# Hybrid decoder layer on one core: the dilated q, k loads on ScalarE's queue, one group's weights loaded a stage earlier, other places for tiles

## Chip, core and metric

One core of a Trainium2 chip runs the whole program. The metric is device microseconds per execution. Engines: TensorE (PE, matmuls; PEld its weight loads), VectorE (DVE), ScalarE (ACT), GpSimd (POOL) and SyncE (SP, which only issues DMAs here). ScalarE and GpSimd also issue DMAs, each in its own instruction order.

## The reference

A decoder layer on x (1 x 1024 x 1024, float32):

```
h     = rms_norm(x, norm_mix_g);  proj = h @ w_in          # 1024 x 5896
dil   = proj[..., :2304]  as (q, k, v) x 3 groups x 4 heads x 64
fox   = proj[..., 2304:3840] as (q, k, v) x 8 heads x 64;  f_logit = next 8 columns + b_fgt
gates = sigmoid(the last 2048 columns + b_gate)
o_a   = three dilated causal window attentions (window, dilation) = (128,1), (512,4), (2048,16),
        with ALiBi bias, merged by a softmax over their log denominators
o_b   = causal attention with logits q.k/8 + c_t - c_s,  c = cumsum(log_sigmoid(f_logit))
x     = x + (g_a * (o_a @ w_dil_out) + g_b * (o_b @ w_fox_out)) @ w_out
gu    = rms_norm(x, norm_ffn_g) @ w_ffn_in                  # 2 x 2816 columns
x     = x + (silu(gu[..., :2816]) * gu[..., 2816:]) @ w_ffn_down
out   = rms_norm(x, norm_final_g)
```

## The kernel before

Every large matmul is done as three: operands are split into a high and a low part (`split`, L94: a copy on ScalarE, L95, and a subtraction on VectorE, L96), and `mm3` (L98) adds hi x hi, hi x lo and lo x hi in PSUM. A weight thus goes through a DMA into a raw tile (two buffers, tag "wr"), then ScalarE, then VectorE, then TensorE.

The stages, in order of time in the profile:

- 0 to 67 us, "foxv" (L349): x is loaded in 8 tiles of 128 rows, normalized (`norm_transpose`), transposed on TensorE and split into hT; `values` (L370) computes the fox values of one tile behind.
- 67 to 140, "dilv" (L424): weights w0 (dilated values of group 0 and the 8 forget columns, 264 columns) and w12 (groups 1 and 2, 512 columns) are loaded, split, and multiplied with the 8 row tiles, group 0 first; the staging tile `st` is stored to DRAM from ScalarE. Beside it, VectorE forms sums of quarters of hT (`form`, behind the last split of w12).
- 140 to 267, "proj" (L490): six calls of `projections`, each two columns blocks by a 2 x 2 block product with seven `prod` of 12 matmuls (L268) instead of eight. `left_side` (L254) makes its left operands: A1 and A22 are splits of raw weights; S12 and S34 are splits of sums that GpSimd forms in the tile `s`. `decay` (L452) turns the forget columns into the cumulated log gates.
- to about 511, "fox" (L535): fox attention, four head pairs. q and k lie in `ql`, `qx`, `kx` (two tiles of 4 KB each, one buffer).
- to 656, "dila" (L777): dilated attention in four units (head pair u, half b). `dil_qk` (L660) loads q, k of three groups, six tiles of 4 KB with one buffer each, from DRAM; `dil_scores` computes scores (L338, by `turns`) and VectorE adds the bias (L689 to L709); `dil_values` does exponentials (L739 to L745), values (L769) and denominators (L772), one unit behind.
- Filler: `ahead` (L214), 24 projections of 48 matmuls into two PSUM banks of their own, evacuated by ScalarE (L224); 8 for dilated q, k (L645), 16 for the gates (L793). They have no tie to the attention and are put wherever TensorE is free. The last one is tied behind the last dilated value matmul.
- then the merge (L802), w_out, the second norm, the first FFN product ("first", 2 plain column blocks, and from 881 "up", L954, 20 block products by `left_side`, `prod`), and the down projection.

The order on each engine is fixed before the run: the library's planner simulates the program with its own cost estimates and emits each engine's instructions in the order in which they became ready there, earlier program text first. At run time every engine works strictly in that order; an instruction that waits for a semaphore holds all behind it, DMA issues too. Memory is a stack of pools: a pool opened later takes the bytes of a closed one, tiles in the order of their first use, and a tile waits only for the users of earlier tiles on its own bytes. So in "proj" the tile `s` came to lie on w12, and in "dila" the six q, k tiles on ql, qx and kx.

Of the kernel before, what the change touches and what calls it, by code (L numbers as in the profile page):

```python
# [8 lines left out]
F32 = mybir.dt.float32  # L9
# [6 lines left out]
P = 128  # L16
# [31 lines left out]
def layer_kernel(  # L48
# [194 lines left out]
        nc.sync.dma_start(out=t[:], in_=src.rearrange("(k p) c -> p k c", p=P))  # L243
        return t

    def pair_of(raw, k=KT, pool=None, tag="w", bufs=2):

        pool = pool or wpool
        w = Pair(pool.tile([P, k, P], F32R, tag=tag + "h", name=nm("wh"), bufs=bufs),
                 pool.tile([P, k, P], F32R, tag=tag + "l", name=nm("wl"), bufs=bufs))  # L250
        split(w.hi[:], w.lo[:], raw)
        return w

    def left_side(pool, rg, ru, bufs):  # L254

        g1, g2, u1, u2 = rg[:, :4], rg[:, 4:], ru[:, :4], ru[:, 4:]
        A1 = pair_of(rg[:])
        s12 = pool.tile([P, KT, P], F32, tag="s", name=nm("s12"), bufs=2)
        nc.gpsimd.tensor_tensor(out=s12[:, :4], in0=u1, in1=u2, op=ALU.add)  # L259
        nc.gpsimd.tensor_tensor(out=s12[:, 4:], in0=s12[:, :4], in1=g1, op=ALU.subtract)  # L260
        S12 = pair_of(s12[:], KT, pool, "s12", bufs)
        s34 = pool.tile([P, KT, P], F32, tag="s", name=nm("s34"), bufs=2)
        nc.gpsimd.tensor_tensor(out=s34[:, :4], in0=g1, in1=u1, op=ALU.subtract)
        nc.gpsimd.tensor_tensor(out=s34[:, 4:], in0=g2, in1=s12[:, 4:], op=ALU.subtract)
        S34 = pair_of(s34[:], KT, pool, "s34", 1)
        return A1, S12, S34, pair_of(u2, 4, pool, "a22", 2)

    def prod(bank, a, b, first=False):  # L268
        for k in range(4):
# [5 lines left out]
    def projections(pool, T, c, dst, dls, sc):  # L275

        T1, T2, T3, T4 = T
        A1, S12, S34, A22 = left_side(pool, *[raw_w(w_in[:, c0:c0 + P]) for c0 in c], 1)
        b1, b2, b3 = pd(), pd(), pd()
        o1, o2 = [pool.tile([P, dl, S // dl], F32, tag="qo", name=nm("qo"), bufs=3) for dl in dls]  # L280
        n1, n2 = [HALF // dl for dl in dls]
        cc, v2, v3 = [pool.tile([P, HALF], F32, tag=n, name=nm(n), bufs=1) for n in ("cc", "v2", "v3")]

        def copy(out, bank, r=1):
            nc.scalar.activation(out=out, in_=view(bank[:], r), func=AF.Copy, scale=sc)

        def join(out, bank, other, r=1):
            p, q = view(bank[:], r), view(other[:], r)
            if sc == 1.0:
                nc.vector.tensor_tensor(out=out, in0=p, in1=q, op=ALU.add)  # L290
            else:
                nc.vector.scalar_tensor_tensor(out=out, in0=p, scalar=sc, in1=q, op0=ALU.mult, op1=ALU.add)

        flat = view(cc[:], 1), view(v2[:], 1), view(v3[:], 1)
        prod(b1, A1[:, :4], B11, True)
        copy(flat[0], b1)
        prod(b2, S12[:, 4:], T2, True)
        join(flat[1], b2, cc)
        prod(b1, A1[:, 4:], B21)
        copy(o1[:, :, :n1], b1, dls[0])  # L300
        prod(b2, S34[:, :4], T3)
        join(flat[2], b2, cc)
        prod(b3, S12[:, :4], T1, True)
        join(o2[:, :, n2:], b3, v3, dls[1])
        prod(b2, A22, T4)
        join(o2[:, :, :n2], b2, cc, dls[1])
        prod(b3, S34[:, 4:], B22)
        join(o1[:, :, n1:], b3, v2, dls[0])
        for o, d in zip((o2, o1), dst[::-1]):
            nc.gpsimd.dma_start(out=d, in_=o[:].rearrange("p r i -> p (r i)"))  # L310
# [35 lines left out]

    lf = cpool.tile([P, NT, 8], F32, name="lf")
    negc = cpool.tile([P, NT, 8], F32, name="negc")
    with pool_of("foxv", 2) as vpool:  # L349
        xts = []  # L350

        def load_x():
            i = len(xts)
            if i < NT:
                xts.append(vpool.tile([P, D], F32, tag="xt", name=nm("xt"), bufs=4))
                nc.sync.dma_start(out=xts[i][:], in_=x[i * P:(i + 1) * P, :])

        load_x()
        gain1 = load_gain(vpool, norm_mix_g)
        nc.gpsimd.memset(ones[:], 1.0)  # L360
        bg = cpool.tile([P, 16], F32, name="bg")
        bf = cpool.tile([P, 8], F32, name="bf")
        nc.gpsimd.dma_start(out=bf[0:1, :], in_=b_fgt[0:1, :])
        with nc.allow_non_contiguous_dma("per-partition gate bias"):
            nc.gpsimd.dma_start(out=bg[:], in_=b_gate[0].rearrange("(k p) -> p k", p=P))
        nc.gpsimd.partition_broadcast(bf[:], bf[0:1, :])
        wv = load_w(w_in[:, FOX0 + 2 * FOX_W:FGT0], KT, FOX_W, tag="wv", bufs=1, pool=vpool,
                    chunk=P, rpool=vpool, rbufs=3, shared=2 * P, between=load_x)

        def values(i):  # L370
            hh, c = divmod(i * P, HALF)
            st = vpool.tile([P, FOX_W], F32, tag="vst", name=nm("vst"), bufs=2)
            n = 256 if i < 2 else FOX_W
            for c0 in range(0, FOX_W, n):
                pv = pd()
                for k in range(KT):
                    mm3(pv[:, :n], hT[hh][:, k, c:c + P], wv[:, k, c0:c0 + n], k == 0, k == KT - 1)
                nc.vector.tensor_copy(st[:, c0:c0 + n], pv[:, :n])
            nc.gpsimd.dma_start(out=vf_dram[i], in_=st[:])

        for i in range(NT):
            load_x()
            hh, c = divmod(i * P, HALF)
            norm_transpose(xts[i][:], gain1, hT[hh], c, vpool, False)
            if i > 0:
                values(i - 1)
        values(NT - 1)


    with pool_of("comb1", 1) as tpool:  # L390
# [31 lines left out]


        with pool_of("dilv", 1) as vpool:  # L424
            w12 = Pair(*[vpool.tile([P, KT, 512], F32R, name=nm("wv"), bufs=1) for _ in range(2)])
            w0 = Pair(*[vpool.tile([P, KT, 264], F32R, name=nm("wv"), bufs=1) for _ in range(2)])
            for w, cols in ((w0, [(2 * DIL_W, 128, 0), (2 * DIL_W + 128, 128, 128), (FGT0, 8, 256)]),
                            (w12, [(2 * DIL_W + 256 + i * P, P, i * P) for i in range(4)])):
                for c0, n, at in cols:
                    raw = wpool.tile([P, KT, n], F32, tag="wr" if n == P else "wf", name=nm("wr"), bufs=2 if n == P else 1)  # L430
                    nc.sync.dma_start(out=raw[:], in_=w_in[:, c0:c0 + n].rearrange("(k p) c -> p k c", p=P))
                    last = split(w.hi[:, :, at:at + n], w.lo[:, :, at:at + n], raw[:])
            for g0, w, n in ((0, w0, 264), (1, w12, 512)):
                for tt in range(NT):
                    pv = pd()
                    for k in range(KT):
                        st = hT_all[:, k, tt * P:(tt + 1) * P] if g0 == 0 else hT_all[:, k, tt::8]
                        mm3(pv[:, :n], st, w[:, k, :n], k == 0, k == KT - 1)
                    st = vpool.tile([P, 512], F32, tag="vst", name=nm("vst"), bufs=2)
                    m = n // 256 * 256  # L440
                    nc.scalar.activation(out=st[:, :m], in_=pv[:, :m], func=AF.Copy)
                    if g0 == 0:
# [5 lines left out]
            with tc.issue_after(last.ins):  # L448
                form(0)
                form(2)  # L450

        def decay(cums):  # L452

            upper = cums.tile([P, P], F32, name="upper", bufs=1)
            nc.gpsimd.memset(upper[:], 1.0)
            nc.gpsimd.affine_select(out=upper[:], in_=upper[:], compare_op=ALU.is_ge, fill=0.0, base=0,
                                    pattern=[[1, P]], channel_multiplier=-1)

            az = cums.tile([P, NT * 8], F32, name="az", bufs=1)
            u = cums.tile([P, NT * 8], F32, name="u", bufs=1)  # L460
            t1 = cums.tile([P, NT * 8], F32, name="t1", bufs=1)
            z = lf[:].rearrange("p a b -> p (a b)")
            nc.vector.tensor_scalar(out=t1[:], in0=z, scalar1=-1.0, scalar2=None, op0=ALU.mult)
            nc.vector.tensor_tensor(out=az[:], in0=z, in1=t1[:], op=ALU.min)
# [9 lines left out]
                                           op0=ALU.min, op1=ALU.subtract)  # L474

            pc = pd()
            nc.tensor.matmul(pc[:, 0:64], upper[:], z, start=True, stop=True)
            nc.tensor.matmul(pc[:, 64:128], ones[:], z, start=True, stop=True)
            tot = cums.tile([P, NT, 8], F32, name="tot", bufs=1)
            nc.vector.tensor_copy(tot[:], pc[:, 64:128].rearrange("p (a b) -> p a b", a=NT))  # L480
            for i in range(1, NT - 1):
                nc.vector.tensor_tensor(out=tot[:, i, :], in0=tot[:, i, :], in1=tot[:, i - 1, :], op=ALU.add)
# [5 lines left out]


        with pool_of("proj", 1) as upool:  # L490
            for pr in range(0, 4, 2):
                for a in range(2):
                    c0 = FOX0 + a * FOX_W + pr * P
                    projections(upool, T, (c0, c0 + P), [fqk_dram[a, pr + i] for i in range(2)], (1, 1), 1.0)
                if pr == 0:
                    decay(upool)
            for two in TWOS:
                projections(upool, T, [dil_cols(*t) for t in two], [dqk_dram[t] for t in two],
                            [STR[a][g] for u, g, a in two], (SCALE, 1.0)[two[0][2]])
# [149 lines left out]
    with pool_of("dil", 1) as spool:  # L649
# [10 lines left out]
        def dil_qk(pool, u):  # L660

            qk = [[None, None] for _ in range(3)]
            for g in range(3):
                for a in range(2):
                    qk[g][a] = pool.tile([P, STR[a][g], S // STR[a][g]], F32, tag=f"qk{g}{a}", name=nm("dqk"), bufs=1)
                    nc.sync.dma_start(out=qk[g][a][:].rearrange("p r i -> p (r i)"), in_=dqk_dram[u, g, a])
            return qk

        def dil_scores(pool, qk, u, b):
# [405 lines left out]
```

## Time and profile before

| | us |
|---|---|
| three runs | 1534.6, 1535.2, 1528.62 (median 1534.6) |
| profiled execution | 1528.89 |
| its span | 1527.0 |
| PE busy | 1472.8 (96%) |
| DVE busy | 893.3 (59%) |
| ACT busy | 537.0 (35%) |
| POOL busy | 418.9 (27%) |

PE's mean granted clock is 0.992. Times in the rows below are microseconds from the span's start. A bracket at the end of a timeline row is the idle time of that engine just before it and what ended it.

### The profile page before, as it was taken

What the parts mean: (1) busy time and instruction counts of PE and PEld (TensorE: products, weight loads), DVE (VectorE), ACT (ScalarE), POOL (GpSimd) and SP (SyncE); (2) the same over time, 40 slices, a digit from 0 to 9 for tenths busy, and PEclk for the clock granted to TensorE, in tenths of its full rate; (3) what the DMA queues carried; (4) which work ended last, traced back from release to release, by engine and by line L of the source; (5) the groups of instructions that cost most, each with busy time, mean ns of one, the idle gap of its engine ahead of it and who ended that gap; (6) DMA issues with size and microseconds to landing.
All of it is one profiled execution on the core that took longest, in us unless ns stands there. A gap on an engine that the chain in (4) does not pass through costs nothing.

```text
span 1527.0 us, 18124 instructions
## 1 busy us (share of the span) xinstructions
PE 1472.8 (96%) x6956; PEld 1191.4 (78%) x6956; DVE 893.3 (59%) x1321; ACT 537.0 (35%) x808; POOL 418.9 (27%) x351
## 2 busy tenths in 40 slices
PE   7999999999999999789999999999999999999997
PEld 6898888866777777568888778888878876888886
DVE  6481533398898399836628854444444445856546
ACT  5232222476566232335315432222222225312113
POOL 1001431263353011100000245555555553140000
PEclk9999999999999999989999999999999999999999
DMA  7232233833332732155613122222222225642302
GB/s 221 70 104 62 92 102 111 248 97 100 112 113 69 255 111 76 56 177 181 242 55 138 42 69 83 83 83 83 83 83 83 83 97 194 206 138 83 97 15 96
DMA packets 139045, 171.60 MB, mean 112 GB/s; under 512 B 6992, under 2 KB 108368, under 8 KB 138960
## 3 DMA queue, kind: packets, MB, share of 16 engines
q1 hardware_dynamic: 119824, 112.25, 24.6%
q0 software_dynamic: 9616, 34.62, 6.0%
q10 hardware_dynamic: 9520, 23.60, 4.2%
q8 instruction: 54, 0.88, 0.2%
q14 instruction: 31, 0.25, 0.1%
HBM read 123.25 MB, written 47.19 MB: 112 GB/s over the span
## 4 chain that ended last, share of the span: by engine, by line
PE 83%; DMA 4%; DVE 4%; ACT 4%; POOL 3%; issue 2%; SPq 0%; ACTq 0%; POOLq 0%; DVEq 0%
PE pd L272 25%; PE pd L101 10%; PE pd L100 10%; PE pd L99 10%; PE pf L99 5%; PE pf L101 5%; PE pf L100 5%; DMA wr<-in_w_ffn_in_dram 2%; PE pd L623 2%; ACT wh L95 2%; PE pd L189 2%; PE pd L190 2%; PE pd L193 2%; POOL sg L983 1%; PE pd L769 1%
## 5 line engine op out<-in xcount | busy, mean ns | idle before, releaser
L95 ACT ACTIVATE wh<-wr 128x1024 fp32r<-128x1024 f32 (+2 forms) x152 | 140.6, 932 | 328.8 <-PE pd L100 92.9
L96 DVE TENSOR_TENSOR wl<-wr,wh 128x1024 fp32r<-128x1024 f32 (+2 forms) x152 | 165.9, 1095 | 151.5 <-ACT wh L95 151.1
L272 PE MATMUL pd<-hT_t,wh 128*128 128x512 f32 x784 | 242.3, 390 | 3.0 <-ACT c L966 2.4
L272 PE MATMUL pd<-tT,wh 128*128 128x512 f32 x672 | 207.0, 389 | 2.5 <-ACT wh L95 2.1
L272 PEld LDWEIGHTS pd<-hT_t,wh 128*128 128x128 f32 x784 | 147.0, 188 | 34.1 <-ACT c L966 2.8
L272 PE MATMUL pd<-hT_t,wl 128*128 128x512 f32 x392 | 154.0, 394 | 1.6 <-DVE wl L96 1.4
L99 PE MATMUL pf<-hT_t,wh 128*128 128x512 f32 x384 | 151.4, 394 | 0.6 <-ACT fst L224 0.6
L101 PE MATMUL pf<-hT_t,wl 128*128 128x512 f32 x384 | 150.9, 393 | 0.0
L100 PE MATMUL pf<-hT_t,wh 128*128 128x512 f32 x384 | 150.6, 392 | 0.0
L272 PEld LDWEIGHTS pd<-tT,wh 128*128 128x128 f32 x672 | 126.0, 188 | 29.5 <-ACT wh L95 2.6
L99 PE MATMUL pd<-wh,wh 128*128 128x512 f32 x352 | 138.1, 393 | 3.8 <-DVE acc L1026 2.5
L259 POOL TENSOR_TENSOR s<-wr 128x512 f32<-128x512 f32 x26 | 41.0, 1575 | 358.1 <-DMA wr<-in_w_ffn_in_dram 260.5
L101 PE MATMUL pd<-wh,wl 128*128 128x512 f32 x352 | 137.6, 391 | 0.0
L100 PE MATMUL pd<-wl,wh 128*128 128x512 f32 x352 | 137.5, 391 | 0.0
L272 PE MATMUL pd<-tT,wl 128*128 128x512 f32 x336 | 130.1, 390 | 0.1
L1026 DVE TENSOR_TENSOR acc<-pd,acc 128x512 f32<-128x512 f32 x128 | 85.8, 686 | 69.0 <-PE pd L101 68.8
L96 DVE TENSOR_TENSOR wl<-s,wh 128x1024 fp32r<-128x1024 f32 x52 | 64.7, 1246 | 63.9 <-ACT wh L95 63.9
L95 ACT ACTIVATE wh<-s 128x1024 fp32r<-128x1024 f32 x52 | 55.1, 1059 | 125.3 <-POOL s L260 93.1
L272 PEld LDWEIGHTS pd<-hT_t,wl 128*128 128x128 f32 x392 | 73.6, 188 | 22.3 <-DVE wl L96 7.3
L99 PEld LDWEIGHTS pf<-hT_t,wh 128*128 128x128 f32 x384 | 72.1, 188 | 20.4 <-issue 4.2
L101 PEld LDWEIGHTS pf<-hT_t,wl 128*128 128x128 f32 x384 | 72.1, 188 | 20.3 <-issue 5.7
L100 PEld LDWEIGHTS pf<-hT_t,wh 128*128 128x128 f32 x384 | 72.1, 188 | 17.3 <-issue 3.0
(220 smaller groups left out, 2770.1 us busy)
## 6 DMA issues: line engine op xcount, KB each, us to landing
wr<-in_w_in_dram SPq DMA_DIRECT2D x46, 512.0 KB, 4.3
wr<-in_w_ffn_in_dram SPq DMA_DIRECT2D x44, 512.0 KB, 4.2
wr<-a_dram SPq DMA_DIRECT2D x22, 512.0 KB, 4.3
wr<-in_w_ffn_down_dram SPq DMA_DIRECT2D x22, 512.0 KB, 3.8
a_dram<-a POOLq DMA_DIRECT2D x20, 512.0 KB, 4.9
qraw<-fqk_dram SPq DMA_DIRECT2D x32, 256.0 KB, 4.1
g_dram<-fst ACTq DMA_DIRECT2D x16, 512.0 KB, 2.8
land<-g_dram SPq DMA_DIRECT2D x16, 512.0 KB, 3.4
```

Source lines behind the costliest of these rows:

```text
L95: nc.scalar.activation(out=hi, in_=src, func=AF.Copy)
L96: return nc.vector.tensor_tensor(out=lo, in0=src, in1=hi.bitcast(F32), op=ALU.subtract)
L99: nc.tensor.matmul(psum, w.hi, m.hi, start=start, stop=False)
L100: nc.tensor.matmul(psum, w.hi, m.lo, start=False, stop=False)
L101: last_mm[0] = nc.tensor.matmul(psum, w.lo, m.hi, start=False, stop=stop)
L189: nc.tensor.matmul(pt[hh][:], w.hi[:, k], m.hi, start=(k == 0), stop=False)
L190: nc.tensor.matmul(pt[hh][:], w.hi[:, k], m.lo, start=False, stop=False)
L193: nc.tensor.matmul(pt[hh][:], w.lo[:, k], m.hi, start=False, stop=(k == kt - 1))
L259: nc.gpsimd.tensor_tensor(out=s12[:, :4], in0=u1, in1=u2, op=ALU.add)
L272: last_mm[0] = nc.tensor.matmul(bank[:], p, q, start=first and k == 0 and n == 0, stop=k == 3 and n == 2, skip_group_check=True)
L623: nc.tensor.matmul(po[half[e], HALF - width[j]:], vf[:, j, pr, e], L[:, off[j]:off[j + 1]], start=(j == nj - 1), stop=(j == 0), skip_group ...
L1026: nc.vector.tensor_tensor(out=acc[:, t, cs], in0=pt[:], in1=acc[:, t, cs], op=ALU.add)
```

## The change

The q, k loads of the dilated attention are issued by ScalarE instead of SyncE. The tile pair w0 gets a pool of its own at the other end of the memory, opened before the first stage, and is loaded (by the new helper `load_wv`) after the norm of row tile 5 in the first stage; the pool closes after the dilated values. In "dilv" the two staging tiles come first, then w12. In `left_side` the pairs S34 and A22 are allocated before the others; in `projections` the output and work tiles come before the left side; the decay's tiles are allocated at the head of "proj", and its matrix of ones is a second half of the tile `sums`.

```
-    def pair_of(raw, k=KT, pool=None, tag="w", bufs=2):
+    def pair_of(raw):
...
     def left_side(pool, rg, ru, bufs):
+        def pair(k, tag, bufs):
+            return Pair(*[pool.tile([P, k, P], F32R, tag=tag + n, name=nm("w" + n), bufs=bufs) for n in "hl"])
+        def fill(w, raw):
+            split(w.hi[:], w.lo[:], raw)
+            return w
         g1, g2, u1, u2 = rg[:, :4], rg[:, 4:], ru[:, :4], ru[:, 4:]
-        A1 = pair_of(rg[:])
+        S34, A22, A1 = pair(KT, "s34", 1), pair(4, "a22", 2), pair_of(rg[:])
         s12 = pool.tile([P, KT, P], F32, tag="s", name=nm("s12"), bufs=2)
...
-        S12 = pair_of(s12[:], KT, pool, "s12", bufs)
+        S12 = fill(pair(KT, "s12", bufs), s12[:])
...
-        S34 = pair_of(s34[:], KT, pool, "s34", 1)
-        return A1, S12, S34, pair_of(u2, 4, pool, "a22", 2)
+        return A1, S12, fill(S34, s34[:]), fill(A22, u2)
...
     def projections(pool, T, c, dst, dls, sc):
         T1, T2, T3, T4 = T
-        A1, S12, S34, A22 = left_side(pool, *[raw_w(w_in[:, c0:c0 + P]) for c0 in c], 1)
-        b1, b2, b3 = pd(), pd(), pd()
         o1, o2 = [pool.tile([P, dl, S // dl], F32, tag="qo", name=nm("qo"), bufs=3) for dl in dls]
         n1, n2 = [HALF // dl for dl in dls]
         cc, v2, v3 = [pool.tile([P, HALF], F32, tag=n, name=nm(n), bufs=1) for n in ("cc", "v2", "v3")]
+        A1, S12, S34, A22 = left_side(pool, *[raw_w(w_in[:, c0:c0 + P]) for c0 in c], 1)
+        b1, b2, b3 = pd(), pd(), pd()
...
+    w0_ctx = pool_of("w0", 1, side="right")
+    w0pool = w0_ctx.__enter__()
+    def load_wv(w, cols):
+        for c0, n, at in cols:
+            raw = wpool.tile([P, KT, n], F32, tag="wr" if n == P else "wf", name=nm("wr"), bufs=2 if n == P else 1)
+            nc.sync.dma_start(out=raw[:], in_=w_in[:, c0:c0 + n].rearrange("(k p) c -> p k c", p=P))
+            last = split(w.hi[:, :, at:at + n], w.lo[:, :, at:at + n], raw[:])
+        return last
...
             norm_transpose(xts[i][:], gain1, hT[hh], c, vpool, False)
+            if i == NT - 3:
+                w0 = Pair(*[w0pool.tile([P, KT, 264], F32R, name=nm("w0"), bufs=1) for _ in range(2)])
+                load_wv(w0, [(2 * DIL_W, 128, 0), (2 * DIL_W + 128, 128, 128), (FGT0, 8, 256)])
...
         with pool_of("dilv", 1) as vpool:
+            sts = [vpool.tile([P, 512], F32, name=nm("vst"), bufs=1) for _ in range(2)]
             w12 = Pair(*[vpool.tile([P, KT, 512], F32R, name=nm("wv"), bufs=1) for _ in range(2)])
-            w0 = Pair(*[vpool.tile([P, KT, 264], F32R, name=nm("wv"), bufs=1) for _ in range(2)])
...
+            last = load_wv(w12, [(2 * DIL_W + 256 + i * P, P, i * P) for i in range(4)])
...
-                    st = vpool.tile([P, 512], F32, tag="vst", name=nm("vst"), bufs=2)
+                    st = sts[tt % 2]
...
+        w0_ctx.__exit__(None, None, None)
-        def decay(cums):
+        def decay(sums, az, u, t1, tot):
...
         with pool_of("proj", 1) as upool:
+            cums = [upool.tile([P] + d, F32, name=n, bufs=1) for n, d in (
+                ("sums", [2, P]), ("az", [NT * 8]), ("u", [NT * 8]), ("t1", [NT * 8]), ("tot", [NT, 8]))]
...
             for g in range(3):
                 for a in range(2):
                     qk[g][a] = pool.tile([P, STR[a][g], S // STR[a][g]], F32, tag=f"qk{g}{a}", name=nm("dqk"), bufs=1)
-                    nc.sync.dma_start(out=qk[g][a][:].rearrange("p r i -> p (r i)"), in_=dqk_dram[u, g, a])
+                    nc.scalar.dma_start(out=qk[g][a][:].rearrange("p r i -> p (r i)"), in_=dqk_dram[u, g, a])
```

## Rows read from the trace of the kernel before

**Rows 1.** Stages: stretch, its us, busy us (instructions) by engine, clock, DMA share, GB/s.

```profile
66.74:139.90 73.16, 70.96 (x385) 70.51 (x384) 37.20 (x41) 19.75 (x28) 0.54 (x1) 1.00 0.29 87
139.90:151.80 11.90, 9.01 (x37) 6.51 (x36) 6.41 (x12) 5.28 (x9) 5.44 (x6) 1.00 0.41 112
...
500.00:524.50 24.50, 24.50 (x115) 16.34 (x113) 4.42 (x7) 3.97 (x6) 3.27 (x4) 1.00 0.94 341
524.50:639.00 114.50, 113.06 (x755) 84.71 (x754) 103.38 (x169) 35.62 (x52) 13.42 (x8) 1.00 0.25 83
...
892.00:1270.00 378.00, 375.97 (x1640) 306.46 (x1640) 162.70 (x196) 106.64 (x135) 208.41 (x152) 1.00 0.26 82
```

**Rows 2.** TensorE's waits: line, releaser, us in total, times, longest.

```profile
PE pd L769 <- ACT L L745: 9.2, 1, 9.2
...
PE pd L272 <- ACT c L966: 2.4, 1, 2.4
PE pd L272 <- ACT wh L95: 2.1, 1, 2.1
PE pd L100 <- DVE wv L96: 2.0, 1, 2.0
```

**Rows 3.** Timeline of SP, ScalarE, VectorE: load and split of w0 (start, us, instruction).

```profile
14.93 3.22 SPq L431 DMA_DIRECT2D wr<-in_w_in_dram  x2
...
57.03 2.15 ACT L95 ACTIVATE wv<-wr 128x1024 fp32r<-128x1024 f32 x3
...
67.55 2.48 DVE L96 TENSOR_TENSOR wv<-wr,wv 128x1024 fp32r<-128x1024 f32 x3
```

**Rows 4.** Stretches of the first stage, columns as in rows 1.

```profile
30.00:50.00 20.00, 20.00 (x106) 16.75 (x105) 13.85 (x27) 8.49 (x19) 1.84 (x4) 1.00 0.13 49
50.00:66.74 16.74, 16.74 (x79) 13.91 (x79) 3.96 (x6) 3.91 (x7) 1.41 (x3) 1.00 0.12 47
```

**Rows 5.** Timeline: last evacuation of group 0, first GpSimd sum, VectorE's S12 split.

```profile
97.08 0.37 ACT L441 ACTIVATE vst<-pd 128x256 f32<-128x256 f32 x1
...
140.16 1.29 POOL L259 TENSOR_TENSOR s<-wr 128x512 f32<-128x512 f32 x1 [71.69 <-PE pd L101]
...
148.60 1.23 DVE L96 TENSOR_TENSOR wl<-s,wh 128x1024 fp32r<-128x1024 f32 x1 [0.42 <-ACT wh L95]
```

**Rows 6.** Timeline of ScalarE: the A22 split at the start of "up".

```profile
885.73 0.63 ACT L95 ACTIVATE wh<-wr 128x512 fp32r<-128x512 f32 x1 [7.40 <-DMA a_dram<-a]
```

**Rows 7.** Timeline of SP's issues around the dilated q, k loads (L666).

```profile
499.96 0.37 SPq L118 DMA_DIRECT2D wr<-in_w_in_dram  x1
500.50 3.29 SPq L666 DMA_DIRECT2D dqk<-dqk_dram  x6
...
541.06 1.76 SPq L666 DMA_DIRECT2D dqk<-dqk_dram  x4
...
557.09 1.05 SPq L666 DMA_DIRECT2D dqk<-dqk_dram  x2
```

**Rows 8.** Tiles ql and dqk (instructions, landing of loads), and timeline rows of PE, DVE.

```profile
L573 PE MATMUL pd<-ql,kx x96: 274/368/397, 294.9 to 479.0; 128*128 128x512 f32 x48, 128*128 128x256 f32 x32, 128*128 128x384 f32 x16
...
DMA to landing us min/median/max: 3.2/5.9/8.9
...
524.49 2.03 PE L338 MATMUL pd<-dqk,dqk 64*128 64x128 f32 x32
...
499.85 1.33 DVE L612 TENSOR_TENSOR Mx<-Mx,L 128x384 f32<-128x384 f32 x3
```

**Rows 9.** TensorE after its longest wait: a stretch (busy, clock, DMA), value matmuls 648-656, 594-601.

```profile
648.00:650.00 2.00, 1.76 (x9) 0.50 0.00 0
...
L769 PE MATMUL pd<-L,vd 128*64 128x128 f32 (+2 forms) x64 | 6.8, 388 | 9.2 <-ACT L L745 9.2
...
L769 PE MATMUL pd<-L,vd 128*64 128x128 f32 (+2 forms) x64 | 4.5, 298 | 0.0
```

**Rows 10.** Timeline of ScalarE: first exponentials of the dilated stage.

```profile
547.15 0.26 ACT L740 ACTIVATE L<-L 128x64 f32<-128x64 f32 x1 [12.95 <-DVE L L736]
```

More of the change, by code (lines that the diff above doesn't have):

```diff
@@ L244, in raw_w @@
         return t
-    def pair_of(raw, k=KT, pool=None, tag="w", bufs=2):
-        pool = pool or wpool
-        w = Pair(pool.tile([P, k, P], F32R, tag=tag + "h", name=nm("wh"), bufs=bufs),
-                 pool.tile([P, k, P], F32R, tag=tag + "l", name=nm("wl"), bufs=bufs))
+    def pair_of(raw):
+        w = Pair(*[wpool.tile([P, KT, P], F32R, tag="w" + n, name=nm("w" + n), bufs=2) for n in "hl"])
         split(w.hi[:], w.lo[:], raw)
@@ L424, in layer_kernel @@
         with pool_of("dilv", 1) as vpool:
+            sts = [vpool.tile([P, 512], F32, name=nm("vst"), bufs=1) for _ in range(2)]
             w12 = Pair(*[vpool.tile([P, KT, 512], F32R, name=nm("wv"), bufs=1) for _ in range(2)])
-            w0 = Pair(*[vpool.tile([P, KT, 264], F32R, name=nm("wv"), bufs=1) for _ in range(2)])
[L427 to L432, printed above, removed]
+            last = load_wv(w12, [(2 * DIL_W + 256 + i * P, P, i * P) for i in range(4)])
             for g0, w, n in ((0, w0, 264), (1, w12, 512)):
@@ L450, in layer_kernel @@
                 form(2)
-        def decay(cums):
-            upper = cums.tile([P, P], F32, name="upper", bufs=1)
-            nc.gpsimd.memset(upper[:], 1.0)
-            nc.gpsimd.affine_select(out=upper[:], in_=upper[:], compare_op=ALU.is_ge, fill=0.0, base=0,
+        w0_ctx.__exit__(None, None, None)
+        def decay(sums, az, u, t1, tot):
+            nc.gpsimd.memset(sums[:], 1.0)
+            nc.gpsimd.affine_select(out=sums[:, 0], in_=sums[:, 0], compare_op=ALU.is_ge, fill=0.0, base=0,
                                     pattern=[[1, P]], channel_multiplier=-1)
-            az = cums.tile([P, NT * 8], F32, name="az", bufs=1)
-            u = cums.tile([P, NT * 8], F32, name="u", bufs=1)
-            t1 = cums.tile([P, NT * 8], F32, name="t1", bufs=1)
             z = lf[:].rearrange("p a b -> p (a b)")
@@ L476, in decay @@
             pc = pd()
-            nc.tensor.matmul(pc[:, 0:64], upper[:], z, start=True, stop=True)
-            nc.tensor.matmul(pc[:, 64:128], ones[:], z, start=True, stop=True)
-            tot = cums.tile([P, NT, 8], F32, name="tot", bufs=1)
+            nc.tensor.matmul(pc[:, 0:64], sums[:, 0], z, start=True, stop=True)
+            nc.tensor.matmul(pc[:, 64:128], sums[:, 1], z, start=True, stop=True)
             nc.vector.tensor_copy(tot[:], pc[:, 64:128].rearrange("p (a b) -> p a b", a=NT))
@@ L495, in layer_kernel @@
                 if pr == 0:
-                    decay(upool)
+                    decay(*cums)
             for two in TWOS:
```

## The prediction

> **What bounds the kernel now.** I read the busy shares by stage first, then TensorE's waits, then the queues around the two longest. The stages [rows 1] show TensorE as the bound nearly everywhere: 375.97 of 378 us in the long product stage 892 to 1270, so no edit there can give anything. What can be had are holes. Of TensorE's waits [rows 2] the change touches four: 9.2 us before the last dilated values (L769), 2.4 us at the first product of the later block-product stage, and 2.1 and 2.0 us in the first 150 us. Two other long ones, at the very start and at the merge, lie on paths that it leaves alone.
>
> The median of the runs is 1534.6 us, but the three runs lie at 1528.62, 1534.6 and 1535.2, and the profiled execution took 1528.89 us (span 1527.0 and 1.9 around it). All durations below are of that execution, so the sum is made against 1528.89; the profile does not show where the other 5.7 us come from.
>
> **1. Weights of dilated group 0 loaded in the first stage.** Before, the last split of these weights stands on VectorE behind the last evacuation of the first stage: three L96 at 67.55, 2.48 us [rows 3], and TensorE waits for them in the group's first matmuls [rows 2]. In 66.74 to 139.9 TensorE is busy 70.96 of 73.16 us [rows 1], so the whole hole is 2.2 us. The three DMAs went out from SP by 18.2 us already [rows 3], among the loads of x; now they are issued after the last of these, so SP's queue is not held by them. What moves is 2.15 us of ScalarE (L95 x3) and 2.48 us of VectorE into the first stage, where VectorE has 3.96 busy of 16.74 us in 50 to 66.74 and 13.85 of 20 in 30 to 50, and TensorE no hole in either [rows 4]: the cover is the matmuls of the values. If the splits fall earlier they could push the norm chain by their own 2.5 us; a gain beyond the hole is excluded, since TensorE is full from 30 on. I take -2.2 (between -2.2 and +0.3). The weights of groups 1 and 2 come earlier too, because their raw buffers are free sooner; TensorE did not wait for them: 0.
>
> **2. Other places for the tiles in the first block products.** GpSimd's first sum (L259) waits 71.69 us for TensorE's last L101, until 140.16 [rows 5], and the split of that sum holds TensorE [rows 2]. The reason is bytes: the sums lie where the weights of groups 1 and 2 lay, which TensorE reads to the end. In the new order of allocation those bytes go to the small tiles, the output tiles, S34 and A22, and the sums and S12 lie behind them, on the bytes of group 0's weights, whose last evacuation is at 97.08 [rows 5], 43 us earlier. So four sums of 1.3 us and the S12 split (1.23 us on VectorE, one before it on ScalarE) are done beside the values. What is late next: S34, whose split still waits for the end at 139.9, needs two times some 1.2 us and is wanted after three products of 12 matmuls at 375.97/1640 = 0.229 us [rows 1], at 148: covered. The hole is 11.90 less 9.01 = 2.89 us [rows 1]; I take -2.8 (between 0, should the sums stay late, and -2.9). The decay's small tiles move to a staging tile whose store ends earlier; its work lies beside TensorE's products before and after: 0, and were it in front of the S12 split it could give back up to the 2.8.
>
> **3. The same order in the later block products.** There `left_side` changes too. Before, ScalarE's split of A22 waits 7.40 us for the store of `a`, until 885.73 [rows 6], and the copy of c1 behind it holds TensorE 2.4 us [rows 2]. By the order of allocation A22 moves off those bytes and the low half of S12 moves onto them. The store's landing then gates VectorE's S12 split (1.23 us, to 886.9) in place of ScalarE. If the planner puts the second b1 product first, as before, TensorE loses some 0.6 us (the c1 copy, by the A22 split of the same shape, 0.63 [rows 6]); if S12 is first, about 1.9. I take -1.0 (between -0.4 and -1.8).
>
> **4. Dilated q, k issued from ScalarE.** The large term. Before, SP issues the first six loads at 500.50, right behind a weight load that it could issue only at 499.96 [rows 7]. The bytes they need are those of ql, qx and kx (six tiles of 4 KB at the same place), last read by L573 at 479.0 [rows 8]. So about 21 us go by in SP's queue. The loads land in at most 8.9 us, yet TensorE's first L338 stands at 524.49, behind more filler [rows 8]. VectorE is busy 4.42 of 24.5 us in 500 to 524.5 and then 103.38 of 114.5 until 639 [rows 1]: from there the dilated work is VectorE's chain, and TensorE fills with gate projections until they run out (one is held back on purpose). Then it stands 9.2 us for the exponentials of the last unit (L745) [rows 2], and with the clock granted at half when it goes on, the 64 value matmuls take 6.8 us instead of 4.5: 2.3 us more [rows 9]. Another 114.5 - 113.06 = 1.4 us are lost before 639 [rows 1]. Together 12.9 us.
>
> From ScalarE the loads can go at about 480, so they land by 495; VectorE is free at 501.2 [rows 8], so its chain can start 15 us or more earlier. The filler does not vanish: what is not run before 524 is run later, and the last chain ends ahead of it. 15 is more than 9.2 + 1.4, so the holes close; as the queues are in order and the plan is made from estimates, I leave 2 us for new small waits: -11 (between 0 and -12.9). The cost: twelve issues, by SP's row six in 3.29 us [rows 7], so 6.6 us at most on an engine with 35.62 busy of 114.5 us [rows 1]. The second six wait for the readers of the first (SP issued them at 541.06 and 557.09) [rows 7]. Queued behind them on ScalarE are evacuations of filler, for which TensorE waits, and the exponentials; before 547.15 ScalarE was idle for 12.95 us [rows 10], so at 541 the wait costs nothing. SP's weight loads behind the removed ones waited for VectorE's splits anyway: 0.
>
> **Sum.** 2.2 + 2.8 + 1.0 + 11 = 17.0. From 1528.89 that is 1511.9, from the median 1517.6. As two runs of three were in the upper group and I can't tell which way the new kernel falls, I take the middle, 1515.
>
> **Rivals.**
> A. *The dilated stage gains nothing* (the change doesn't do what it says there). For it: the order on every engine is planned ahead, and the first L338 stood some 12 us behind the landing of its data already; in 500 to 524.5 the DMA engines are busy 0.94 of the time at 341 GB/s [rows 1], so a queue may not have been the limit. Against: at 480 to 495 the six loads would not meet that load, since half of it is theirs. Then 6.0 us remain: 1522.9 or 1528.6, middle 1525.7. The Trainium skill says in "DMA: Bandwidth & Descriptors", section "Issuing engines are not separate DMA queues", that transfers from any issuing engine run on the same 16 DMA engines and that spreading them saves only issue time; by it the fourth term would be 0 and the sum 6. The 0.94 agrees with it for that stretch, but 500.50 against 479.0 is a wait before the issue, of which the rule does not speak.
> B. *Slower: ScalarE is held by its own issues.* If the second six stand together on ScalarE, it is held from 541.06 until 557.09, and the exponentials of 547.15 start 10 us late or more; VectorE's sums and TensorE's values behind them are late by as much, and the filler runs out before. 10.3 less the 6.0 of the other terms is +4.3: 1533.2 or 1538.9. It decides as soon as the hold in front of the exponentials exceeds 6 us. For it: the 16 us between SP's two groups are the wait for L338 to read the rest. Against: the loads went out in two groups, so the planner set them by readiness. In "DMA: Bandwidth & Descriptors", section "Anatomy of one DMA", the Trainium skill says that any semaphore wait happens on the issuing sequencer before dispatch, which makes such a hold possible; SP's rows agree.
>
> **How the numbers follow.** The forecast has 0.58, A 0.25, B 0.12; 0.05 is for what I don't see. The forecast's own range is 1508 (all holes closed, 20 us, from the lower base) to 1523. A reaches to 1529, so the range is 1507 to 1530; above it lies most of B. What a measurement can tell from no change is about 0.5%, 7.7 us: faster means under 1526.9. That holds for nearly all of the forecast and half of A: 0.68. Slower (over 1542.3) needs a hold of some 14 us in front of the exponentials: half of B and a part of the rest, 0.10. Same: 0.22.
>
> **What would show it.** Right: no wait before the group 0 matmuls near 67; GpSimd's first sum near 100 and no L95 wait at the first products; the first dilated loads issued by ScalarE near 480 and the first L338 before 515; no 9 us wait at L769 and no half clock there. Wrong: L338 still near 520, or ScalarE idle in the dilated stage with its own DMA next and TensorE waiting for L224 or L745; a new wait of the norm chain in 20 to 50; S12's split waiting for the store of `a` longer than A22 did.

## The result and the profile after

| | before | after |
|---|---|---|
| median of 9 runs each, side by side | 1534.24 us | 1523.08 us |
| lowest and highest | 1528.62, 1536.84 | 1519.59, 1525.49 |
| profiled execution, its span | 1528.89, 1527.0 | 1522.51, 1520.2 |

The ratio is 0.9935, with a 95% interval of 0.9919 to 0.9952: 11 us less between the medians, 6.4 between the two profiled executions. The time lies inside the stated range of 1507 to 1530, but at the very end of the forecast's own 1508 to 1523 and not where its likeliest case put it: 1515 was 8 us too low, and 1522.9 is what rival A gave from the lower base. The first three steps gave nearly what they were priced at, the fourth, the large one, gave nothing.

The stages of the kernel after, columns as in [rows 1]:

```profile
62.50:137.60 75.10, 75.10 (x406) 74.24 (x405) 38.84 (x41) 19.94 (x28) 7.53 (x8) 1.00 0.24 74
137.60:148.00 10.40, 9.69 (x42) 7.36 (x41) 5.71 (x11) 6.19 (x10) 2.30 (x2) 1.00 0.47 128
496.00:520.50 24.50, 24.50 (x114) 16.37 (x112) 4.27 (x7) 3.97 (x6) 3.28 (x4) 1.00 0.77 265
520.50:634.50 114.00, 112.55 (x754) 84.54 (x753) 102.67 (x168) 35.23 (x51) 13.42 (x8) 1.00 0.29 100
888.00:1263.00 375.00, 372.87 (x1628) 304.10 (x1627) 162.84 (x195) 105.73 (x134) 208.32 (x152) 1.00 0.25 81
```

The 2.2 us hole of the first row is gone, of the 2.9 us in the second 0.7 are left, and the dilated stage from 520.5 shows the numbers of before, four us earlier. TensorE's waits, columns as in [rows 2]:

```profile
PE pd L780 <- ACT L L756: 8.8, 1, 8.8
...
PE pd L276 <- ACT cc L289: 0.7, 1, 0.7
PE pd L276 <- ACT c L977: 0.7, 1, 0.7
```

Of the four waits that the change touches, the longest stands (L780 is before's L769); the copy of c1 costs 0.7 instead of 2.4; the waits for the splits of w0 and S12 are gone, and 0.7 us stay at the second product into b1, behind the copy cc.

The timeline of the early steps (ScalarE, then VectorE in the first stage; GpSimd; ScalarE at 138), against [rows 3, 5]:

```profile
18.94 0.26 ACT L95 ACTIVATE w<-wr 128x64 fp32r<-128x64 f32 x1 [0.15 <-DMA wr<-in_w_in_dram]
...
25.81 1.23 DVE L96 TENSOR_TENSOR w<-wr,w 128x1024 fp32r<-128x1024 f32 x1 [0.58 <-ACT w L95]
...
90.94 1.75 POOL L264 TENSOR_TENSOR s<-wr 128x512 f32<-128x512 f32 x1 [21.79 <-PE pd L101]
92.66 2.26 POOL L268 TENSOR_TENSOR s<-wr,wr 128x512 f32<-128x512 f32 x1
135.14 0.31 POOL L468 MEMSET sums<- 128x256 f32 x1 [40.22 <-DMA vd_dram<-vst]
135.41 1.29 POOL L265 TENSOR_TENSOR s<-s,wr 128x512 f32<-128x512 f32 x1
...
138.05 0.60 ACT L454 ACTIVATE vst<-pd 128x512 f32<-128x512 f32 x1 [5.32 <-PE pd L101]
```

The splits of w0 end at 27 instead of 70. GpSimd's first sum waits for group 0's last matmul, until 90.94, and no longer until 140.16. The second half of the sum still comes late: the decay's fill of `sums`, planned ahead of it, waits 40.22 us for a staging tile's store and holds GpSimd. So S12 is ready only just in time for its product, which still stands behind the second one into b1; whether an earlier S12 would have brought it forward and saved the 0.7 us was not tried.

The start of "up" and the dilated loads, against [rows 6 to 9]:

```profile
875.14 0.61 ACT L95 ACTIVATE wh<-wr 128x512 fp32r<-128x512 f32 x1
...
883.28 1.22 DVE L96 TENSOR_TENSOR wl<-s,wh 128x1024 fp32r<-128x1024 f32 x1 [2.87 <-DMA a_dram<-a]
```

```profile
503.71 0.60 ACT L327 ACTIVATE rc<-pd 128x512 f32<-128x512 f32 x1 [9.52 <-PE pd L637]
...
510.70 1.06 ACT L95 ACTIVATE wh<-wr 128x1024 fp32r<-128x1024 f32 x1 [4.62 <-PE pf L100]
510.94 1.42 ACTq L677 DMA_DIRECT2D dqk<-dqk_dram  x2
512.38 1.90 ACTq L677 DMA_DIRECT2D dqk<-dqk_dram  x4
...
520.57 2.03 PE L342 MATMUL pd<-dqk,dqk 64*128 64x128 f32 x32
...
643.66 7.15 PE L780 MATMUL pd<-L,vd 128*64 128x256 f32 x64 [8.78 <-ACT L L756]
```

A22's split no longer waits; the store of `a` gates VectorE's S12 split instead, without a wait on TensorE that shows. The dilated loads go out at 510.94, ten us *later* than from SyncE. On ScalarE they stand behind the evacuation L327 of the last fox unit and, directly, behind the copy of a filler's weights at 510.70, which had waited 4.62 us for TensorE. The first scores are where they were, shifted by four us, and so are the 8.8 us and the half clock behind them (7.15 us for 64 value matmuls).

### The profile page after: what moved, and what is told of

It reads as the page before. It is cut to its first block, busy times and chain, and to the rows that moved or that the text cites. A ratio compares the mean times of both kernels' runs of the same rounds, so it can differ in the third digit from the quotient of the medians.

```text
span 1520.2 us, 18124 instructions
## 1 busy us (share of the span) xinstructions
PE 1472.8 (97%) x6956; PEld 1192.0 (78%) x6956; DVE 894.1 (59%) x1321; ACT 536.8 (35%) x808; POOL 418.4 (28%) x351
## 4 chain that ended last, share of the span: by engine, by line
PE 85%; DMA 4%; DVE 3%; ACT 3%; POOL 3%; issue 2%; SPq 0%; ACTq 0%; POOLq 0%; DVEq 0%
PE pd L276 26%; PE pd L99 10%; PE pd L100 10%; PE pd L101 10%; PE pf L100 5%; PE pf L101 5%; PE pf L99 5%; DMA wr<-in_w_ffn_in_dram 2%; PE pd L189 2%; PE pd L634 2%; PE pd L190 2%; PE pd L193 2%; ACT wh L95 2%; POOL sg L994 1%; PE pd L780 1%
## 5 line engine op out<-in xcount | busy, mean ns | idle before, releaser
L101 PEld LDWEIGHTS pf<-hT_t,wl 128*128 128x128 f32 x384 | 72.1, 188 | 19.8 <-issue 5.0
```

Of the source, the lines that this page charges most:

```text
L101: last_mm[0] = nc.tensor.matmul(psum, w.lo, m.hi, start=False, stop=stop)
```

## The experiments

All are timed against the kernel before on the same chip; its 52 runs beside them have a median of 1532.0 us.

**E1, only w0's early load and its place.** `before` with the pool at the far end and `load_wv` behind row tile 5.

> Only the first edit: group 0's weights get the tile pair at the far end and are loaded in the first stage; all else as before. Theory 1 (the gain of the changed kernel is the sum of its local holes): the three splits fall between 18 and 26 us, the wait of 2.0 us at group 0's first matmuls is gone, the end of the dilated values moves from 139.7 to 137.6 and everything behind it by the same 2 us; the first block products keep their waits of 2.1 and 0.7 us, the dilated stage its 9 us wait. Time 2 us below the kernel before, run for run. Theory 2 (what the profiles don't show, some 4 to 5 us of the median, is a loss that comes and goes in the kernel before and that this edit removes): more than 5 us below in the median, 2 us between the profiles.

Measured: 1525.8 (12 runs) against 1531.1 (23), ratio 0.9969 [0.9958, 0.9981]. The wait is gone and the others stay (that for the S12 split at 1.4 us), as theory 1 has it. The time is theory 2's: the profile's span is 3.3 us shorter, the median 5.3 and not 2, and the interval leaves 2.9 us at least. So more than the hole went with it.

**E2, only the places.** The changed kernel with `load_wv(w0, ...)` back in "dilv", in front of w12, and the loads on SyncE.

> Only the other places for tiles (staging tiles first, S34 and A22 and the small tiles ahead of the sums, w0 at the far end but loaded where it was loaded before); dilated q, k from SyncE. Theory 1: the wait of 2.0 us at group 0 stays, GpSimd's first sum starts near 93 and not at 140, the 2.1 us wait for the S12 split is gone and 0.7 us stays, and the start of the later block products loses 0.7 instead of 2.4 us: 2.1 + 1.7 + up to 1.0 = 4 to 5 us below the kernel before. Theory 2: the median falls by 8 us or more, that is the unseen part goes with this edit.

Measured: 1523.89 (6 runs), 0.9954 [0.9938, 0.997]. Two misses: the wait at group 0 was expected to stay and went (TensorE is busy all of 66 to 72), and the time is the changed kernel's, 7 us below and not 4 to 5. The splits of w0 fall at the same place as in the changed kernel although the program asks for them a stage later; ScalarE's and VectorE's timelines, then a stretch, columns as in [rows 1]:

```profile
22.82 1.05 ACT L95 ACTIVATE w<-wr 128x1024 fp32r<-128x1024 f32 x1
...
26.36 1.23 DVE L96 TENSOR_TENSOR w<-wr,w 128x1024 fp32r<-128x1024 f32 x1 [0.58 <-ACT w L95]
...
66.00:72.00 6.00, 6.00 (x44) 5.65 (x43) 0.69 (x1) 0.43 (x1) 0.54 (x1) 1.00 0.13 46
```

So a place of its own is enough to bring the splits forward, and the earlier place in the program text is not needed. What held them before was the place in memory, by the order of the pools on bytes of the first stage; whether by a wait or by the planned order, no run separates.

**E3, only ScalarE's queue; E4, the changed kernel without it.** One word each way:

```
-                    nc.sync.dma_start(out=qk[g][a][:]...
+                    nc.scalar.dma_start(out=qk[g][a][:]...
```

> Only the last edit: the kernel before with the twelve dilated q, k loads issued by ScalarE. Theory 1 (the plan puts the loads behind the end of the fox stage, so the other queue changes nothing that TensorE sees): first loads near 515, first dilated score matmuls at 524.5 as before, the 9 us wait before the last values stays, time equal within 1 us. Rival (the loads did gain, and the other edits used it up): first scores earlier than 520 and a wait under 5 us, time 4 us or more below.

> The changed kernel with the twelve loads back on SyncE. Theory 1: loads near 496, all later times as in the changed kernel, the same 8.8 us wait, time equal to the changed kernel within 1 us, so some 6 us (profile to profile) below the kernel before. Rival (ScalarE's queue is worth something, 4 us or more): it is that much slower than the changed kernel, 1526 to 1528.

Measured: E3 1530.69 (12 runs), 0.9998 [0.9983, 1.0014]; E4 1522.23 (6 runs), 0.9947 [0.9932, 0.9963]. Both as theory 1: the queue is worth nothing. In E4 SyncE issues at 497.04 and the first scores stand at 521.04; in E3 ScalarE issues at 515.41, and they stand at 525.04. SyncE's issues and ScalarE's last fox evacuation in E4, then ScalarE's issue in E3:

```profile
467.84 29.03 SPq L118 DMA_DIRECT2D wr<-in_w_in_dram  x3
497.04 3.15 SPq L677 DMA_DIRECT2D dqk<-dqk_dram  x6
...
504.41 0.60 ACT L327 ACTIVATE rc<-pd 128x512 f32<-128x512 f32 x1 [9.52 <-PE pd L637]
```

```profile
515.41 1.16 ACTq L666 DMA_DIRECT2D dqk<-dqk_dram  x2
```

The Trainium skill's rule in "DMA: Bandwidth & Descriptors", section "Issuing engines are not separate DMA queues", which the prediction weighed, gave the fourth term as 0, and 0 was measured. The runs don't test its reason, though: from neither queue did the loads go out before 497.

**E5 and E6, tiles of their own.** ql, qx and kx lie in a pool that stays open until the dilated stage has ended, and the first dilated tiles take them over by tag; all else as after.

```
+    q_ctx = pool_of("foxq", 1)
+    qpool = q_ctx.__enter__()
...
-            qx = [pool.tile([P, S], F32R, tag=f"qx{e}", name=nm("qx"), bufs=1) for e in range(2)]
+            qx = [qpool.tile([P, S], F32R, tag=f"qx{e}", name=nm("qx"), bufs=1) for e in range(2)]
...
-                    qk[g][a] = pool.tile([P, STR[a][g], S // STR[a][g]], F32, tag=f"qk{g}{a}", name=nm("dqk"), bufs=1)
+                    t = qpool.tile([P, S], F32R, tag=("ql", "qx", "kx")[g] + str(a), name=nm("dqk"), bufs=1)
```

> The changed kernel, with ql, qx and kx of the fox attention in a pool of their own that stays open, and the dilated q, k of the first pair taking those tiles over by name; ScalarE issues the loads. Theory 1 (what held the loads is the plan: tiles of a pool that takes over another pool's bytes are placed only when that whole pool has ended, here with the last fox output at 507, though their bytes were last read at 475): the loads go out between 470 and 485, the first dilated scores come 8 to 15 us before 520.6, the wait of 8.8 us before the last values shrinks by as much, to 0 to 2, and the time falls by 7 to 11 us to 1512 to 1516. Rival 1 (the issue was not what held the scores: VectorE's additions into tiles of the closed pool, or the fillers placed ahead, hold the chain): the loads are early, but the last values still wait 7 to 9 us, time within 2 us of the changed kernel. Rival 2 (ScalarE held by its own issues): exponentials of the fox stage late, TensorE waiting for them, slower than 1526.

> The same with the loads from SyncE. Theory 1: the same gain, 1512 to 1516, within 2 us of the run from ScalarE, as the queue is not what counts. If ScalarE's queue is what counts once the tiles are free early (SyncE's weight loads in front wait for VectorE's splits of the fillers): loads only at 490 to 500 and half of the gain or none.

Measured: from ScalarE 1505.62 (4 runs), 0.9823 [0.9801, 0.9845]; from SyncE 1507.23 (5 runs), 0.9831 [0.9808, 0.9853]. ScalarE's issues, then TensorE's timeline in E5; the last row is SyncE's in E6:

```profile
466.85 0.33 ACTq L681 DMA_DIRECT2D dqk<-dqk_dram  x1
...
475.00 0.36 ACTq L681 DMA_DIRECT2D dqk<-dqk_dram  x1
...
501.82 2.03 PE L342 MATMUL pd<-dqk,dqk 64*128 64x128 f32 x32
...
631.68 4.46 PE L784 MATMUL pd<-L,vd 128*64 128x256 f32 x64
```

```profile
466.87 8.27 SPq L681 DMA_DIRECT2D dqk<-dqk_dram  x6
```

The loads go out 44 us earlier than in the changed kernel, from either queue (30 earlier than from SyncE in E4); the scores begin 19 us earlier, at the end of the fox stage; the last values start at 631.68 without a wait and at full clock. The gain is 17 us, beyond the 7 to 11 expected. It splits up: the 8.8 and 2.7 us (7.15 less 4.46) at the last values, 0.85 us less idle time before them (114 less 113.40 against 114 less 112.55), and 1.75 us by which the fox stage ends earlier (its last L327 at 501.96 against 503.71; why, no run shows) make 14.1 of the 14.6 us by which the first merge matmul moves (653.58 against 668.21). The other 1.9 of the 16.5 between the profiles lie further on: in 840 to 850 of the profile after, behind a hole of 1.66 us, the clock is 0.83, which leaves 1.7 us of work for later, and E5 has 1.00 at that place, behind the same hole. The stretch of the changed kernel:

```profile
840.00:850.00 10.00, 8.34 (x39) 6.54 (x38) 8.81 (x9) 2.88 (x5) 0.00 (x0) 0.83 0.00 0
```

**E7 and E8, the kernel before again.**

> The kernel before once more, for a profile. The runs of it so far fall by some 1.5 us for each 0.001 of mean granted clock (0.986 to 0.992, 1537 to 1528 us). Theory 1 (the early holes of the kernel before let the clock be granted at half for some us in part of its runs): in a run at 0.990 or less a stretch of the first 150 us, or at 881 to 890, shows a granted clock clearly below that of the profile shown before, 5 us of loss or more. Rival: the clock is lower by a little everywhere, or only at the starts of the last stages, which the change does not touch.

> The kernel before a third time, for the same question: the same stretches as in the run before it, if its mean granted clock is again 0.990 or less; if it is 0.992, the stretches of the profile shown before.

Measured: 1530.98 at a mean granted clock of 0.990, 1531.73 at 0.991. Four stretches each of the profile shown before, of E7 and of E8, a fence for each, columns as in [rows 1]; the third number from the right is the clock (1.00 is the upper of its two levels, 2.4 GHz):

```profile
66.00:72.00 6.00, 3.80 (x25) 3.23 (x25) 3.09 (x4) 0.00 (x0) 0.54 (x1) 1.00 0.46 124
72.00:78.00 6.00, 6.00 (x52) 6.00 (x51) 2.52 (x3) 2.40 (x3) 0.00 (x0) 1.00 0.55 149
150.00:160.00 10.00, 10.00 (x44) 8.24 (x45) 5.67 (x5) 3.59 (x4) 5.93 (x4) 1.00 0.33 84
890.00:900.00 10.00, 10.00 (x46) 8.28 (x45) 6.21 (x6) 4.16 (x5) 6.31 (x4) 1.00 0.42 113
```

```profile
66.00:72.00 6.00, 3.80 (x25) 3.31 (x24) 3.09 (x4) 0.00 (x0) 0.54 (x1) 0.94 0.52 144
72.00:78.00 6.00, 6.00 (x41) 6.00 (x41) 2.53 (x3) 2.38 (x3) 0.00 (x0) 0.77 0.57 144
150.00:160.00 10.00, 10.00 (x38) 8.14 (x39) 5.73 (x6) 3.86 (x5) 5.63 (x4) 0.84 0.39 100
890.00:900.00 10.00, 10.00 (x46) 8.29 (x45) 6.40 (x6) 3.12 (x4) 5.07 (x3) 1.00 0.40 108
```

```profile
66.00:72.00 6.00, 3.80 (x19) 3.12 (x18) 3.09 (x4) 0.00 (x0) 0.54 (x1) 0.90 0.33 86
72.00:78.00 6.00, 6.00 (x43) 6.00 (x42) 2.53 (x3) 2.39 (x3) 0.00 (x0) 0.81 0.58 151
150.00:160.00 10.00, 9.07 (x39) 7.20 (x40) 6.27 (x7) 3.90 (x6) 4.51 (x4) 1.00 0.39 104
890.00:900.00 10.00, 10.00 (x39) 8.05 (x38) 6.89 (x6) 3.01 (x4) 5.24 (x3) 0.83 0.38 105
```

Behind each of the three early holes (2.0, 2.9 and 2.4 us) the clock stands below 1.00 in some executions and not in others. The count in brackets tells the price: in 72 to 78 E7 starts 41 matmuls instead of 52, that is 1.3 us of work (6 us / 52 each) left for later; in 150 to 160 it is 38 for 44, 1.4 us. In E8 the counts of 72 to 78 and 890 to 900 (43 for 52, 39 for 46) give 1.0 and 1.5 us. That is 2.7 us in E7 and 2.6 in E8, half of the 5 or more that E7's theory expected. In the profile after, the same four stretches all show 1.00. The profile before had its own such stretch elsewhere, 0.91 in 1290 to 1310, as E7 has, where after has 1.00.

**E9, tiles of their own on the kernel before.** The edit of E6 on `before`.

> The kernel before with only the tiles of their own for ql, qx, kx and the dilated q, k of the first pair; loads from SyncE, weights and block products as before. Theory 1 (the held loads cost what the tiles of their own gave back on the changed kernel, independently of the other edits): first dilated scores near 506, no wait of more than 2 us before the last values, and 15 to 18 us below the kernel before, 1514 to 1517; the waits of 2 us at group 0 and of 2 and 0.7 us at the first block products stay. Rival (the gain of 16.6 us on the changed kernel needs the earlier edits, for example through the clock): 8 to 12 us below the kernel before.

Measured: 1517.27 (6 runs) against 1534.32 (11), 0.9894 [0.9873, 0.9916]: 17 us, with the early waits still there. Between the profiles it is 12.4 us, near the rival's 8 to 12, so the medians carry the reading: the ratios of the changed kernel and of E9 multiplied, 0.9935 x 0.9894 = 0.983, are E5's 0.9823. By them the held loads and the early holes are separate costs.

**E10, the fillers' tiles at the far end.** E5 with `pool_of("beside", 1, side="right")`.

> The changed kernel with the tiles of their own (loads from ScalarE), and the pool of the fillers' output tiles (fst) at the far end of the memory. In the run with own tiles the first split of the merge (oh, L95) waited for the store of the last filler's output until 652.5, though its data had been asked for at 641.4, and TensorE stood 5.4 us. Theory 1 (the same mechanism in a second place: the new pool's tiles lie on bytes that are used to the end): without the shared bytes the split starts at 646 to 648, the wait at the first merge matmul falls from 5.4 to under 1 us, the granted clock behind it is full, and the time falls by 4.5 to 7 us to 1499 to 1501. Rival (the loads of the fox outputs land late, not the bytes): the wait stays over 4 us, time within 2 us of 1505.6.

Measured: 1508.11 (4 runs), 0.9831 [0.9808, 0.9854], no faster than E5, where 1499 to 1501 was expected. The merge's wait is gone, but another of the same length has come, which neither theory had. TensorE's waits, then ScalarE's timeline at that place:

```profile
PE pf L99 <- ACT fst L224: 5.5, 1, 5.5
```

```profile
273.24 1.06 ACT L562 ACTIVATE qx<-qraw 128x1024 fp32r<-128x1024 f32 x1 [2.98 <-DMA qraw<-fqk_dram]
279.82 1.06 ACT L562 ACTIVATE kx<-qraw 128x1024 fp32r<-128x1024 f32 x1 [5.51 <-DMA qraw<-fqk_dram]
280.78 0.58 ACT L224 ACTIVATE fst<-pf 128x512 f32<-128x512 f32 x1
```

With the fox pools 11.5 KB lower, the fox q, k conversions stand ahead of a filler's evacuation on ScalarE; they wait for their loads, and the evacuation that TensorE needs waits behind them. That the lower place put them there is inferred. It is what rival B feared of ScalarE's own issues, here from conversions and at another place.

**E11, the merge's tiles in another order.** E5 with the pair that is written later allocated first in "gates", so that it takes the fillers' bytes.

```
+        ohs = {n: Pair(*[mpool.tile([P, n, S], F32R, name=nm(t), bufs=1) for t in ("oh", "ol")]) for n in (2, 4)}
...
-            o = Pair(mpool.tile([P, n, S], F32R, name=nm("oh"), bufs=1),
-                     mpool.tile([P, n, S], F32R, name=nm("ol"), bufs=1))
+            o = ohs[n]
```

> The changed kernel with the tiles of their own (loads from ScalarE), the fillers' output tiles where they were, and in the pool of the merge the pair for the dilated outputs allocated ahead of the pair for the fox outputs, so that the pair that is written first no longer lies on the fillers' output tiles. Theory 1 (bytes): the first split of the merge follows the last filler's evacuation at 649 instead of its store at 652.5, TensorE's wait there falls from 5.4 to about 2 us, the fox stage keeps its order (unlike with the far end), and the time is 3 to 5 us below 1505.6, 1501 to 1503. Rival (as with the far end, what is gained at the merge is lost in another place): within 2 us of 1505.6, and another wait of 3 us or more appears.

Measured: 1502.44 (5 runs) against 1531.02 (9), 0.9812 [0.979, 0.9834], as theory 1 expected and the lowest median of all. Measured against before on its own chip it is not clear of E5, whose interval overlaps; that it is better than E5 rests on the two profiles, spans of 1498.9 and 1503.7 us. ScalarE's split in E5 and in E11 (timelines), then the stretch 640 to 660 of E5 and of E11:

```profile
652.47 2.00 ACT L95 ACTIVATE oh<-land 128x1024 fp32r<-128x1024 f32 x2 [3.40 <-DMA g_dram<-fst]
```

```profile
649.46 3.90 ACT L95 ACTIVATE oh<-land 128x1024 fp32r<-128x1024 f32 x4 [0.40 <-ACT fst L224]
```

```profile
640.00:660.00 20.00, 14.57 (x52) 11.48 (x52) 5.82 (x6) 7.47 (x9) 3.73 (x7) 0.83 0.68 224
```

```profile
640.00:660.00 20.00, 17.52 (x76) 13.84 (x76) 6.41 (x7) 9.57 (x11) 3.73 (x7) 1.00 0.80 275
```

With three us less of waiting the clock stayed at its upper level as well: 76 matmuls instead of 52 in the same 20 us.

## Why the prediction was right and wrong

That the time lies in the range is in part luck: of the 17 us forecast, 11 did not come, and some 5 came between the medians that no term of the sum had.

**Step 1, -2.2: right in size.** TensorE's last matmul of the dilated values, for which GpSimd's sum waited until 140.16 [rows 5], now releases the last evacuation at 138.05: 2.1 us. Its reason was half right: the tile's own place alone is enough to move the splits, without the earlier load in the program (E2). That a gain beyond the hole was excluded was wrong: E1 gave 5.3 us in the median, of which the clock behind the hole (E7, E8) is a likely part.

**Step 2, -2.8: 2.2 came.** The sums left the bytes of w12, as argued. What was missed is named in the prediction as a risk, the decay's work in front of the S12 split: its fill of `sums` holds GpSimd up to 135.4. It did not give the 2.1 us back, and the 0.7 us at cc were there before, within the 2.89 that the prediction took for one hole.

**Step 3, -1.0: -1.7 came.** The store of `a` did gate S12 in place of A22, as the prediction had it, but the products ahead of S12 cover it. The 0.7 us left at the copy of c1 are the 0.6 of the branch with the second b1 product first; the -1.0 was a middle between two branches. Together the three steps have 6.0 by these rows; the profiles differ by 6.4.

**Step 4, -11: nothing came.** The step that failed is the one from "So about 21 us go by in SP's queue" to "From ScalarE the loads can go at about 480". They went out at 510.94, and the first scores stood at 520.57, which the prediction had named as a sign of being wrong. Another queue could not give the loads 480, because the plan had placed them later than that on either one. The chain behind was read rightly: loads at 467 to 475 remove the 9 us wait, the half clock and the small holes [rows 9], and the term's upper end of 12.9 us is about what E5 got back there (8.8, 2.7 and 0.85, and the fox stage's 1.75 on top). What held the loads, E5, E6 and E9 show: in tiles that take over single tiles of a pool still open they go out when the last reader of their bytes is done; in a new pool on the same bytes they stand, in ScalarE's order, behind the last evacuation of the whole fox stage. On SyncE in E4 they go at 497.04, right behind three weight loads and before the fox stage's last L327 at 504.41, so no wait for its end was written into them: the order of the plan was the limit. Why the planner orders by the pool's end is inferred from that order and was not seen by itself. What spoke for it was in the rows: the first L338 stood some 12 us behind the landing of its data [rows 7, 8], so the loads were not what it waited for. Rival A used just this and got 0.25. Three small slips of the prediction bear on nothing: the six tiles (128 x 4 KB each) are 3.1 MB, a good third and not half of the 8.4 MB that 341 GB/s make in 24.5 us [rows 1]; the terms at their best add up to 19.8 us, which leads to 1509 and not 1508; and rival B's 10.3 has no working, from 547.15 to 557.09 it is 9.9.

**The median.** The prediction could not say where the 5.7 us between its profile and the median of before lie. Of the 52 runs of before the span grows by 1.7 us for each 0.001 by which the mean granted clock is lower (from 1526.8 on average at 0.992 to 1534.3 at 0.988, correlation -0.92); their mean clock is 0.990. Much of that slope is mere sums, as 0.001 of 1530 us is 1.5 us. The changed kernel's nine runs lie at 0.992 or 0.993. At 0.992 the spans are 1526.8 before and 1521.0 after, 5.8 us, which is what the holes themselves give. Some 2 of the other 5 us lie in which runs of before were drawn: the nine beside the result have a median of 1534.24, the 52 others 1532.0. The last 3 us fit the clock behind the holes, where E7 and E8 lose 2.7 and 2.6 us at places that the change has closed. That is an estimate from two profiles at 0.990 and 0.991; a run at 0.988 was not profiled, and in which executions the clock falls is open.

**Rival B** did not happen: the second six loads went out at 537 and 551, and the exponentials shifted with the rest.

## What to carry to other kernels

Where tiles share bytes, ask which tile a first write follows: here three of the four waits, and the one at the merge, went or shrank when tiles were given other bytes, and moving the loads to another queue did nothing where their place in memory stayed. Before a late issue is put down to its queue, look whether the instruction had anything to wait for when it got there; if not, the plan put it there, and what moved it here was what the plan knows of (tiles, pools, order of allocation). And a hole on TensorE costs more than its length in some executions, so compare many runs with their mean clock, and read one profile as one draw.

## What was not expected of the hardware

Holes of only 2.0 to 2.9 us on TensorE were followed by stretches with a mean granted clock of 0.77 to 0.84 over 6 to 10 us in some executions (E7, E8) and by 1.00 in others (the profile shown before, E3 behind the same holes). "TensorE: Matmul & The Clock Gate" of the Trainium skill says, in "HAM oscillation — how this bites in real kernels", that waits between groups of matmuls bring the slow clock back. The waits of its example are longer than the holes here, so the rows go beyond it, and they show the slow clock in some executions only.
